# Second feed-forward product of an encoder layer: eight operand layouts and pass orders, chosen by K tile

## The chip, the core and the metric

The kernel runs on one core of a Trainium2 chip. The metric is the device time of one execution in microseconds (us). Before the change two runs gave 2583.47 and 2583.69 us, median 2583.58 us. One further execution was taken with the hardware profiler; its numbers are those of the profile below.

## The reference

One encoder layer on 2048 tokens of width 1024: an input projection, a bidirectional mLSTM group beside a latent attention group, an output projection, and a feed-forward block. Only the last line matters here:

```
h = rms_norm(x, g_ffn_norm[l])
x = x + jnp.square(jax.nn.relu(h @ w_ff1[l])) @ w_ff2[l]
```

`h` is 2048 x 1024, `w_ff1` 1024 x 4096, `w_ff2` 4096 x 1024. All is float32. The change touches the second product alone, the one with `w_ff2`.

## The kernel before, in words

**The program as a whole.** The phases follow one another: input projection, attention with the mLSTM scans woven in, output projection, first feed-forward product (`layer1`), second feed-forward product (`layer2`). Each float32 product is made from three matmuls of a rounded 32-bit type: every operand is split into a high part (a rounded copy, made by ACT, L53) and a low part (the difference, made by DVE, L54), and `mm3` (L68 to L71) issues high x high, high x low and low x high into the same PSUM bank. In the order of arguments of `nc.tensor.matmul(out, a, b)`, `a` is the stationary operand (128 columns, loaded by a LDWEIGHTS of its own) and `b` is the moving operand (up to 512 columns).

**The second product.** It is a seven-product scheme over 2 x 2 blocks of tokens and output columns (`PROD2`), so the main loop of `layer2` runs over `N = 7 * NU = 112` passes, with `NU = 16` K tiles to a product. Pass `n` has the product `i = n // 16` and the K tile `f = n % 16`. In one pass:

- the stationary operands are `uh` and `ul`, the two parts of a 128 x 2 x 512 tile of activations, cut into eight blocks of 128 tokens
- the moving operands are `wh` and `wl`, the two parts of a 128 x 512 tile of weights
- for each block `b` of 0 to 7 `mm3` adds three matmuls to the PSUM bank `pd[b]`; a bank is started in pass `f == 0` and stopped in `f == 15`, so a pass is 24 matmuls of 128 x 512 and a product 384.

**What runs beside it.** `load2(n + 3)` fetches the next raw tiles over SP's DMA queue, `combine2(n + 2)` lets POOL combine weight blocks in some products, and `split2(n + 2)` has ACT and DVE write the two parts of both operands, two passes ahead. The pools `g_u` and `g_w` hold three buffers, so the split for pass `n + 2` waits for the matmuls of pass `n - 1`. After the last pass of a product ACT and DVE copy the eight banks out (L1877, L1875) and DVE adds them to the accumulators (L1838) over the following passes. The order of issue is the order of the Python code here (a manual schedule): no planner moves anything.

**The places that the change touches.** `open2` (L1750) opens the pools and splits passes 0 and 1; `split2` (L1794) splits all later ones; the inner loop of `layer2` (around L1849) issues the matmuls. In all three `uh` and `ul` are tiles of `[P, 2, 512]` each, and `w2h` and `w2l` tiles of `[P, 512]`. Elements of all of them lie one after the other, and every matmul operand is a run of 128 or 512 neighbouring elements.

Of the kernel before, what the change touches and what calls it, by code (L numbers as in the profile page):

```python
# [9 lines left out]
F32R = mybir.dt.float32r  # L10
# [8 lines left out]
P = 128  # L19
# [30 lines left out]
def split(nc, hi, lo, src, g=None, eng=None):  # L50

    if g is None:
        r = nc.scalar.copy(hi, src)  # L53
        (eng or nc.vector).tensor_tensor(lo, src, hi.bitcast(F32), op=ALU.subtract)  # L54
    else:
        r = nc.scalar.activation(hi, src, AF.Copy, scale=g)
        nc.vector.scalar_tensor_tensor(lo, src, g, hi.bitcast(F32), op0=ALU.mult, op1=ALU.subtract)
    return r
# [9 lines left out]
def mm3(nc, out, ah, al, bh, bl, first, last):  # L68
    nc.tensor.matmul(out, ah, bh, start=first, stop=False)  # L69
    nc.tensor.matmul(out, ah, bl, start=False, stop=False)  # L70
    nc.tensor.matmul(out, al, bh, start=False, stop=last)  # L71
# [1378 lines left out]
class FeedForward:  # L1450
# [3 lines left out]
    NU = FF // 256  # L1454
# [295 lines left out]
    def open2(self, ent):  # L1750

        c, pool = self.c, self.c.tc.tile_pool
        self.urp = ent(pool(name="g_ur", bufs=4, reuse_waits="tile"))
        self.wrp = ent(pool(name="g_wr", bufs=4, reuse_waits="tile"))
        self.up = ent(pool(name="g_u", bufs=3, reuse_waits="tile"))
        self.wp = ent(pool(name="g_w", bufs=3, reuse_waits="tile"))
        self.R, self.acc, self.op2 = {}, {}, {}
        for n in range(2):
            r = self.raw2.pop(n)
            uh = self.up.tile([P, 2, 512], F32R, name="uh")  # L1760
            ul = self.up.tile([P, 2, 512], F32R, name="ul")
            wh = self.wp.tile([P, 512], F32R, name="w2h")
            wl = self.wp.tile([P, 512], F32R, name="w2l")
            for g in range(2):
                split(c.nc, uh[:, g, :], ul[:, g, :], r[g])
            split(c.nc, wh, wl, r[2])
            self.op2[n] = uh, ul, wh, wl
# [26 lines left out]
    def split2(self, n):  # L1794
        nc = self.c.nc
        ur, wr = self.raw2.pop(n)
        uh = self.up.tile([P, 2, 512], F32R, name="uh")
        ul = self.up.tile([P, 2, 512], F32R, name="ul")
        wh = self.wp.tile([P, 512], F32R, name="w2h")
        wl = self.wp.tile([P, 512], F32R, name="w2l")  # L1800
        split(nc, uh, ul, ur)
        split(nc, wh, wl, wr)
        self.op2[n] = uh, ul, wh, wl

    def load_acc(self, t):
        a = self.acc[t] = self.ap.tile([P, 2, 512], F32, name=f"acc{t}")
        self.c.nc.sync.dma_start(a.rearrange("p a n -> p (a n)"), self.c.d_x1[t * P:(t + 1) * P, :])
# [20 lines left out]
    def layer2(self, psD):  # L1828
        c, nc = self.c, self.c.nc
        NU = self.NU  # L1830
        N = 7 * NU
        todo = []

        def add(i, b, src, quad):
            a, j = quad
            t = 8 * (b // 4) + 4 * a + b % 4
            dst = self.acc[t]
            nc.vector.tensor_tensor(dst[:, j, :], src, dst[:, j, :], op=ALU.add)  # L1838
            tok = slice(t * P, (t + 1) * P)
            if i == 4:  # L1840
                self.later.append(lambda: nc.sync.dma_start(c.out[tok, :], dst.rearrange("p a n -> p (a n)")))
            elif i > 4:
                self.later.append(lambda: nc.sync.dma_start(c.out[tok, j * 512:(j + 1) * 512], dst[:, j, :]))

        for n in range(N):
            i, f = divmod(n, NU)
            if f == 0:
                pd = [psD.tile([P, 512], F32, name="pd") for _ in range(8)]
            uh, ul, wh, wl = self.op2.pop(n)  # L1849
            for b in range(8):  # L1850
                g, tt = divmod(b, 4)
                ts = slice(tt * P, (tt + 1) * P)
                mm3(nc, pd[b], uh[:, g, ts], ul[:, g, ts], wh, wl, f == 0, f == NU - 1)
            if n + 3 < N:
                self.load2(n + 3)
            if i == 0:
                self.load_acc(f)
            self.flush()
            if n + 2 < N:
                self.combine2(n + 2)  # L1860
                self.split2(n + 2)
            for _ in range(2):
                if todo:
                    todo.pop(0)()
            if f == NU - 1:
                while todo:
                    todo.pop(0)()
                quads = PROD2[i][2]
                for b in range(8):
                    if b % 2 and len(quads) == 1:  # L1870
                        add(i, b, pd[b], quads[0])
                    else:
                        t = c.e[:, b, :]
                        if b % 2:
                            nc.vector.tensor_copy(t, pd[b])  # L1875
                        else:
                            nc.scalar.copy(t, pd[b])  # L1877
                        for quad in quads:
                            todo.append(lambda i=i, b=b, t=t, quad=quad: add(i, b, t, quad))
                    if n == N - 1:  # L1880
                        while todo:
                            todo.pop(0)()
                        self.flush()
# [127 lines left out]
```

## Time and profile before

| what | value |
|---|---|
| median of two runs | 2583.58 us |
| span of the profiled execution, first to last instruction | 2586.2 us |
| PE busy with matmuls | 2567.1 us, 99% of the span |
| matmuls of the second product, out tile `pd` | 3 x 896 = 2688 |
| first of them, last of them starts | 1971.9 us, 2581.4 us |
| DVE, ACT, POOL busy | 1679.2, 1211.0, 402.9 us |

The profiled execution is 2.6 us longer than the median. In the profile PE stands for the matmuls, PEld for the loads of stationary operands, which overlap them. The duration given for one matmul holds its way through the array too, so that neighbouring matmuls overlap: what a matmul costs in a stream is the distance between two starts, its *pitch*. The profile names instructions by line; the matmuls of the second product stand at L69, L70 and L71 with the out tile `pd`.

### The profile page before, as it was taken

Reading aid. Unit: us, or ns where it says so; the run is one execution under the profiler, and the core shown is the slowest. Engines: PE = TensorE matmul, PEld = TensorE weight load, DVE = VectorE, ACT = ScalarE, POOL = GpSimd, SP = SyncE. Lnnn points to the kernel's source line nnn. Section 1 sums busy time; section 2 is a strip of 40 time slices with the busy share of each in tenths; the row PEclk is TensorE's granted clock in tenths of the full one; section 3 lists DMA queues with packets and bytes.
Section 4 is the critical chain, followed back from the end, with each engine's and each line's share of the span. In section 5 each row is a group of like instructions: output and inputs, shape, how many; then the busy total and the mean of one; then the engine's idle time right before and its main releaser. Section 6 shows DMA issues by size and latency. Waiting matters only on the chain. (4 is left out here: it accounts for less than half of the span.)

```text
span 2586.2 us, 37106 instructions
## 1 busy us (share of the span) xinstructions
PE 2567.1 (99%) x13232; PEld 2170.3 (84%) x13232; DVE 1679.2 (65%) x3206; ACT 1211.0 (47%) x2457; POOL 402.9 (16%) x438
## 2 busy tenths in 40 slices
PE   9999999999999999999999999999999999999999
PEld 7888888888888888898888888888888888888887
DVE  5585467666676667675448777877775577676443
ACT  5454444546656566561135554655554323332332
POOL 1211111023224224121000000000000233232000
PEclk9999999999999999999999999999999999999999
DMA  5434234356455555336675655744446644444652
GB/s 172 144 118 143 91 119 145 81 137 133 96 95 122 88 119 96 88 109 185 200 242 174 200 192 191 255 167 143 163 142 250 242 144 146 147 147 147 211 177 96
DMA packets 297757, 391.57 MB, mean 151 GB/s; under 512 B 32677, under 2 KB 186340, under 8 KB 297572
## 3 DMA queue, kind: packets, MB, share of 16 engines
q1 hardware_dynamic: 295108, 384.74, 49.7%
q10 hardware_dynamic: 2464, 4.46, 0.5%
q8 instruction: 104, 1.70, 0.3%
q14 instruction: 81, 0.66, 0.1%
HBM read 256.94 MB, written 132.17 MB: 150 GB/s over the span
## 5 line engine op out<-in xcount | busy, mean ns | idle before, releaser
L69 PE MATMUL pd<-w2h,uh 128*128 128x512 f32 x896 | 348.7, 389 | 0.1
L71 PE MATMUL pd<-w2h,ul 128*128 128x512 f32 x896 | 348.6, 389 | 0.0
L70 PE MATMUL pd<-w2l,uh 128*128 128x512 f32 x896 | 348.5, 389 | 0.0
L54 DVE TENSOR_TENSOR ul<-ur,uh 128x1024 fp32r<-128x1024 f32 x110 | 144.4, 1312 | 248.7 <-ACT uh L53 248.4
L53 ACT CAST uh<-ur 128x1024 fp32r<-128x1024 f32 x110 | 115.9, 1054 | 395.5 <-PE pd L70 381.0
L54 DVE TENSOR_TENSOR ptl<-ptp,pth 128x512 fp32r<-128x512 f32 x252 | 173.5, 689 | 171.5 <-ACT pth L53 166.5
L53 ACT CAST pth<-ptp 128x512 fp32r<-128x512 f32 x252 | 146.3, 582 | 244.9 <-PE ptp L1120 228.6
L1629 DVE TENSOR_TENSOR e<-pu,e 128x512 f32<-128x512 f32 x224 | 151.0, 687 | 96.0 <-PE pu L71 94.0
L1080 DVE TENSOR_SCALAR_CACHE_REDUCE p<-ps 128x512 f32<-128x512 f32 x256 | 174.6, 682 | 53.5 <-PE ps L1079 42.6
L69 PEld LDWEIGHTS pd<-w2h,uh 128*128 128x128 f32 x896 | 168.2, 188 | 35.4 <-DVE e L1629 0.5
L71 PEld LDWEIGHTS pd<-w2h,ul 128*128 128x128 f32 x896 | 168.2, 188 | 35.0
L70 PEld LDWEIGHTS pd<-w2l,uh 128*128 128x128 f32 x896 | 168.2, 188 | 34.9
L1789 POOL TENSOR_TENSOR r<-wr,r 128x512 f32<-128x512 f32 x48 | 92.2, 1920 | 614.5 <-DMA wr<-in_w 599.2
L1120 PE MATMUL ptp<-ident,p 128*128 128x128 f32 x1008 | 151.3, 273 | 0.7 <-ACT p L1091 0.7
L69 PE MATMUL pz<-wh,hh 128*128 128x512 f32 (+1 forms) x384 | 149.9, 392 | 2.1 <-ACT hh L53 1.1
L71 PE MATMUL pz<-wh,hl 128*128 128x512 f32 (+1 forms) x384 | 150.3, 391 | 0.0
L70 PE MATMUL pz<-wl,hh 128*128 128x512 f32 (+1 forms) x384 | 149.7, 391 | 0.1
L70 PE MATMUL pv<-ptl,vh 128*128 128x256 f32 x496 | 140.8, 284 | 2.3 <-DVE ptl L54 1.9
L69 PE MATMUL pv<-pth,vh 128*128 128x256 f32 x496 | 140.6, 284 | 0.4 <-ACT pth L53 0.4
L71 PE MATMUL pv<-pth,vl 128*128 128x256 f32 x496 | 140.3, 283 | 0.0
L1632 ACT ACTIVATE e<-e 128x512 f32<-128x512 f32 x128 | 81.0, 633 | 124.0 <-DVE e L1629 117.2
L1091 ACT ACTIVATE p<-p,nm 128x2048 f32<-128x2048 f32 x64 | 128.6, 2009 | 20.8 <-DVE nm L1084 20.2
(470 smaller groups left out, 6561.8 us busy)
## 6 DMA issues: line engine op xcount, KB each, us to landing
d_u<-e SPq DMA_DIRECT2D x224, 256.0 KB
ur<-d_u SPq DMA_DIRECT2D x110, 512.0 KB
wr<-in_w SPq DMA_DIRECT2D x96, 256.0 KB
w1raw<-in_w SPq DMA_DIRECT2D x42, 512.0 KB
raw<-in_w_in SPq DMA_DIRECT2D x48, 256.0 KB
r<-in_w SPq DMA_DIRECT2D x22, 512.0 KB
mb<-d_M SPq DMA_DIRECT2D x32, 256.0 KB
r<-in_x SPq DMA_DIRECT2D x16, 512.0 KB
```

What stands on the lines that cost most here:

```text
L53: r = nc.scalar.copy(hi, src)
L54: (eng or nc.vector).tensor_tensor(lo, src, hi.bitcast(F32), op=ALU.subtract)
L69: nc.tensor.matmul(out, ah, bh, start=first, stop=False)
L70: nc.tensor.matmul(out, ah, bl, start=False, stop=False)
L71: nc.tensor.matmul(out, al, bh, start=False, stop=last)
L1080: nc.vector.tensor_scalar(probs[b, a][:, j, :], o, SCALE, None, op0=ALU.mult, op1=ALU.max, accum_out=maxes[b, a][:, j:j + 1])
L1091: nc.scalar.activation(p, p, AF.Exp, bias=maxes.pop((b, a)), accum_out=dens[b][:, a:a + 1])
L1120: nc.tensor.transpose(pt[:, k, :], p[:, j, k * P:(k + 1) * P], c.ident)
L1629: nc.vector.tensor_tensor(out, o, t, op=ALU.add)
L1632: nc.scalar.activation(t, t, AF.Relu)
L1789: nc.gpsimd.tensor_tensor(R, wr, R, op=ALU.subtract)
```

## The change

The two parts of an activation tile now lie in one tile `u2` of 2064 elements to a partition (8256 bytes, where two tiles of 4096 bytes stood before), and each part of a weight tile in a tile of 528 elements (2112 bytes, before 2048). The K tile `f` picks a variant `v = f // 2`, 0 to 7, so each variant has 2 of the 16 passes of every product: 14 passes, 336 matmuls. The variants differ in one thing each:

| v | K tiles | what is different |
|---|---|---|
| 0 | 0, 1 | high part first, low part behind it, as runs of 1024 elements |
| 1 | 2, 3 | moving operand read from its last element to its first, and the PSUM output written in reverse too |
| 2 | 4, 5 | order within the pass: all eight blocks high x high, then all eight low x high, then all eight high x low |
| 3 | 6, 7 | high and low part interleaved element by element: both are written, and the stationary operand is read, with a step of 2 |
| 4 | 8, 9 | activation tile begins 8 elements (32 bytes) further on |
| 5 | 10, 11 | weight tiles begin 32 bytes further on |
| 6 | 12, 13 | weight tiles begin 4 elements (16 bytes) further on |
| 7 | 14, 15 | order within a block: high x low, high x high, low x high |

Its core:

```diff
     def split2(self, n):
         nc = self.c.nc
         ur, wr = self.raw2.pop(n)
-        uh = self.up.tile([P, 2, 512], F32R, name="uh")
-        ul = self.up.tile([P, 2, 512], F32R, name="ul")
-        wh = self.wp.tile([P, 512], F32R, name="w2h")
-        wl = self.wp.tile([P, 512], F32R, name="w2l")
+        v = n % self.NU // 2
+        uh, ul = self.place_u(v)
+        wh, wl = self.place_w(v)
         split(nc, uh, ul, ur)
         split(nc, wh, wl, wr)
         self.op2[n] = uh, ul, wh, wl
+
+    def place_u(self, v):
+
+        u = self.up.tile([P, 2064], F32R, name="u2")
+        if v == 3:
+            u = u[:, 0:2048].rearrange("p (g t a) -> p a g t", a=2, g=2)
+        else:
+            o = 8 if v == 4 else 0
+            u = u[:, o:o + 2048].rearrange("p (a g t) -> p a g t", a=2, g=2)
+        return u[:, 0], u[:, 1]
+
+    def place_w(self, v):
+
+        o = {5: 8, 6: 4}.get(v, 0)
+        return [self.wp.tile([P, 528], F32R, name=f"w2{part}")[:, o:o + 512] for part in "hl"]
+
+    def multiply2(self, n, pd):
+
+        nc, NU = self.c.nc, self.NU
+        f = n % NU
+        v = f // 2
+        uh, ul, wh, wl = self.op2.pop(n)
+        todo = []
+        for b in range(8):
+            g, tt = divmod(b, 4)
+            ts = slice(tt * P, (tt + 1) * P)
+            ah, al, o = uh[:, g, ts], ul[:, g, ts], pd[b]
+            bh, bl = wh, wl
+            if v == 1:
+                bh, bl, o = bh[:, ::-1], bl[:, ::-1], o[:, ::-1]
+            todo.append(((o, ah, bh), (o, ah, bl), (o, al, bh)))
+        order = [(b, i) for b in range(8) for i in range(3)]
+        if v == 2:
+            order = [(b, i) for i in (0, 2, 1) for b in range(8)]
+        elif v == 7:
+            order = [(b, i) for b in range(8) for i in (1, 0, 2)]
+        first, last = set(), {}
+        for b, i in order:
+            last[b] = i
+        for b, i in order:
+            nc.tensor.matmul(*todo[b][i], start=f == 0 and b not in first, stop=f == NU - 1 and last[b] == i)
+            first.add(b)
...
-            uh, ul, wh, wl = self.op2.pop(n)
-            for b in range(8):
-                g, tt = divmod(b, 4)
-                ts = slice(tt * P, (tt + 1) * P)
-                mm3(nc, pd[b], uh[:, g, ts], ul[:, g, ts], wh, wl, f == 0, f == NU - 1)
+            self.multiply2(n, pd)
```

`open2` gets the same two calls with `v = 0`. The number of instructions on every engine stays as it was; all matmuls of the second product now stand at one line, L1841, and those on the high and on the low part both read the tile `u2`.

On PE the first pass of variant 2 (K tile 4 of the first product) stands like this before. A row is line, operation, out tile, moving tile, stationary tile; `pd_20120` to `pd_20127` are the eight banks:

```order
L69 MATMUL pd_20120<-w2h_20236,uh_20234 128x512
L70 MATMUL pd_20120<-w2l_20237,uh_20234 128x512
L71 MATMUL pd_20120<-w2h_20236,ul_20235 128x512
L69 MATMUL pd_20121<-w2h_20236,uh_20234 128x512
L70 MATMUL pd_20121<-w2l_20237,uh_20234 128x512
L71 MATMUL pd_20121<-w2h_20236,ul_20235 128x512
```

And now, around the end of the second group of eight and the start of the third (the banks are `pd_20118` to `pd_20125`):

```order
L1841 MATMUL pd_20123<-w2h_20231,u2_20230 128x512
L1841 MATMUL pd_20124<-w2h_20231,u2_20230 128x512
L1841 MATMUL pd_20125<-w2h_20231,u2_20230 128x512
L1841 MATMUL pd_20118<-w2l_20232,u2_20230 128x512
L1841 MATMUL pd_20119<-w2l_20232,u2_20230 128x512
L1841 MATMUL pd_20120<-w2l_20232,u2_20230 128x512
```

Every matmul now goes to another bank than the one before it, and the moving tile changes once in the pass instead of sixteen times.

The first pass of variant 7 (K tile 14 of the first product) on PE, before:

```order
L69 MATMUL pd_20120<-w2h_20616,uh_20614 128x512
L70 MATMUL pd_20120<-w2l_20617,uh_20614 128x512
L71 MATMUL pd_20120<-w2h_20616,ul_20615 128x512
L69 MATMUL pd_20121<-w2h_20616,uh_20614 128x512
L70 MATMUL pd_20121<-w2l_20617,uh_20614 128x512
```

and now (`x2` are two such rows in a row):

```order
L1841 MATMUL pd_20118<-w2l_20602,u2_20600 128x512
L1841 MATMUL pd_20118<-w2h_20601,u2_20600 128x512 x2
L1841 MATMUL pd_20119<-w2l_20602,u2_20600 128x512
L1841 MATMUL pd_20119<-w2h_20601,u2_20600 128x512 x2
L1841 MATMUL pd_20120<-w2l_20602,u2_20600 128x512
```

The matmul with the low part of the weights comes first in each block; the banks are still finished one after the other.

More of the change, by code (lines that the diff above doesn't have):

```diff
@@ L1759, in open2 @@
             r = self.raw2.pop(n)
-            uh = self.up.tile([P, 2, 512], F32R, name="uh")
-            ul = self.up.tile([P, 2, 512], F32R, name="ul")
-            wh = self.wp.tile([P, 512], F32R, name="w2h")
-            wl = self.wp.tile([P, 512], F32R, name="w2l")
+            uh, ul = self.place_u(0)
+            wh, wl = self.place_w(0)
             for g in range(2):
@@ L1796, in split2 @@
         ur, wr = self.raw2.pop(n)
[L1797 to L1800, printed above, removed]
+        v = n % self.NU // 2
+        uh, ul = self.place_u(v)
+        wh, wl = self.place_w(v)
         split(nc, uh, ul, ur)
```

## The prediction

> **What bounds the kernel now.** I read the first page of the profile, then the view of the tile `pd`, then the timeline of one pass. The page comes first; its rows end with busy time, mean duration in ns, and the engine's idle time before such instructions:
>
> ```profile
> span 2586.2 us, 37106 instructions
> PE 2567.1 (99%) x13232; PEld 2170.3 (84%) x13232; DVE 1679.2 (65%) x3206; ACT 1211.0 (47%) x2457; POOL 402.9 (16%) x438
> L69 PE MATMUL pd<-w2h,uh 128*128 128x512 f32 x896 | 348.7, 389 | 0.1
> L71 PE MATMUL pd<-w2h,ul 128*128 128x512 f32 x896 | 348.6, 389 | 0.0
> L70 PE MATMUL pd<-w2l,uh 128*128 128x512 f32 x896 | 348.5, 389 | 0.0
> ```
>
> PE is busy for 99% of the span, and its 2688 matmuls of the second product were preceded by 0.1 us of idle time in all. Nothing that ACT, DVE, POOL or the DMAs do in this stage is late. How fast the matmuls stream is read from the view of `pd` (durations min/median/max in ns, then the first and last start):
>
> ```profile
> L69 PE MATMUL pd<-w2h,uh x896: 389/389/494, 1971.9 to 2580.9; 128*128 128x512 f32 x180
> L71 PEld LDWEIGHTS pd<-w2h,ul x896: 187/188/188, 1972.2 to 2581.2; 128*128 128x128 f32 x180
> L71 PE MATMUL pd<-w2h,ul x896: 388/389/397, 1972.4 to 2581.4; 128*128 128x512 f32 x180
> ```
>
> From the first start, 1971.9, to the last, 2581.4, are 2687 steps in 609.5 us: a pitch of 226.8 ns. A pass of 24 takes 5.44 us, and the 336 matmuls of one variant 76.2 us. The timeline inside one pass shows the same pitch without exception:
>
> ```profile
> 2100.18 0.39 PE L69 MATMUL pd<-w2h,uh 128*128 128x512 f32 x1
> 2100.19 0.19 PEld L70 LDWEIGHTS pd<-w2l,uh 128*128 128x128 f32 x1
> 2100.41 0.39 PE L70 MATMUL pd<-w2l,uh 128*128 128x512 f32 x1
> 2100.41 0.19 PEld L71 LDWEIGHTS pd<-w2h,ul 128*128 128x128 f32 x1
> 2100.64 0.39 PE L71 MATMUL pd<-w2h,ul 128*128 128x512 f32 x1
> 2100.64 0.19 PEld L69 LDWEIGHTS pd<-w2h,uh 128*128 128x128 f32 x1
> 2100.86 0.39 PE L69 MATMUL pd<-w2h,uh 128*128 128x512 f32 x1
> ```
>
> So the stage is a stream of matmuls with nothing between them. It changes its time only if the pitch of some matmuls changes, or if a split comes so late that PE waits. The granted clock gives no room; in this stretch PE, PEld, DVE and ACT (us, and counts), clock, DMA share and GB/s were:
>
> ```profile
> 2000.00:2100.00 100.00, 100.00 (x443) 82.81 (x442) 2.47 (x4) 2.35 (x4) 1.00 0.62 219
> ```
>
> **What a matmul's pitch is made of.** In the attention part matmuls of 256 columns stream, each with its own load of 128 columns:
>
> ```profile
> 1101.70 0.28 PE L69 MATMUL pv<-pth,vh 128*128 128x256 f32 x1
> ...
> 1102.89 0.28 PE L70 MATMUL pv<-ptl,vh 128*128 128x256 f32 x1
> ```
>
> Ten steps lie between these two, 1.19 us, a pitch of 119 ns. Another 256 columns cost 226.8 - 119 = 107.8 ns, so 0.421 ns a column: of the 226.8 ns, 215.6 ns are 512 columns and 11.2 ns are fixed. This gives a ceiling for any gain: if every matmul of the stage lost its whole fixed part, 2688 x 11.2 ns = 30.1 us, 1.2%. Faster by 2% (51.7 us) would need columns to go through faster, and every variant still moves 512 columns a matmul.
>
> **The change part by part**
>
> *Splits (all variants, and the step of 2 in variant 3).* One round of them, ACT and DVE (in brackets the idle time before and what ended it):
>
> ```profile
> 2102.88 1.05 ACT L53 CAST uh<-ur 128x1024 fp32r<-128x1024 f32 x1 [3.87 <-PE pd L70]
> 2103.96 1.23 DVE L54 TENSOR_TENSOR ul<-ur,uh 128x1024 fp32r<-128x1024 f32 x1 [1.32 <-ACT uh L53]
> 2105.11 1.78 DVE L54 TENSOR_TENSOR w2l<-r,w2h 128x512 fp32r<-128x512 f32 x1
> 2108.32 1.05 ACT L53 CAST uh<-ur 128x1024 fp32r<-128x1024 f32 x1 [3.87 <-PE pd L70]
> ```
>
> The round begins when the old pass has let go of its buffers, at 2102.88, and ends at 2106.89; it serves the pass two further on, which begins two passes, 10.88 us, after the start of the round: 6.9 us of slack. With `uh` and `ul` in one tile the release comes one matmul later (the last reader is then the low part), 0.23 us. If the step of 2 in variant 3 made the ACT copy and the DVE difference on 1024 elements four times as long, 3.15 and 3.69 us more, the round would still end inside its slack if nothing piled up, and only two passes in sixteen do it. Cost: 0, hidden behind 10.88 us of matmuls; without that cover it would be at most those 6.84 us in each of 14 passes, 96 us.
>
> *Orders (variants 2 and 7).* Each neighbourhood that they make has its kind in the timeline above: L69 to L70 keeps the stationary operand and changes the moving one, L70 to L71 changes both, L71 to L69 keeps the moving tile and changes bank and stationary operand. The starts lie 0.23, 0.23 and 0.22 us apart, rounded. So neither a change of bank nor one of the moving tile has a price here; 336 x 2 x 0 = 0. The read-out after K tile 15 meets the banks in the old sequence, since variant 7 still finishes block by block. The end of the kernel stays as it is, too: last matmul, read-out, last addition.
>
> *Start addresses and tile pitch (variants 4, 5, 6; and all variants, through the larger tiles).* No matmul operand of the trace is known by its row to begin 16 or 32 bytes off, but the rows do show pitches that differ with the place of the operands. In `layer1`, same shape:
>
> ```profile
> 1707.17 0.39 PE L69 MATMUL pu<-h0h,r 128*128 128x512 f32 x1
> ...
> 1709.74 0.39 PE L71 MATMUL pu<-h0h,r 128*128 128x512 f32 x1
> 1452.21 0.39 PE L71 MATMUL pu<-h2h,w1raw 128*128 128x512 f32 x1
> ...
> 1454.25 0.39 PE L71 MATMUL pu<-h2h,w1raw 128*128 128x512 f32 x1
> ```
>
> The first pair spans 11 steps, 233.6 ns each; the second 9 steps, 226.7 ns each. Moving tiles of the same pool, stationary tiles of another pool: 6.9 ns. That is the upper bound for a bad place: 336 x 6.9 ns = 2.3 us for each variant, 18.5 us if the larger tiles did it to all 2688. The lower bound is 0 for three of these, since 226.7 is the lower of the two pitches, or the fixed 11.2 ns at the very best, 3.8 us a variant. I take 0: the new tiles lie in the same pools in the same sequence, shifted by some hundred bytes, far nearer to the old ones than one pool is to another.
>
> *Stationary operand with a step of 2 (variant 3).* How long the load of an operand streams follows from two widths:
>
> ```profile
> L759 PEld LDWEIGHTS pm<-v,kw 128*64 128x64 f32 x240 | 12.5, 136 | 5.0 <-issue 5.0
> L71 PEld LDWEIGHTS pv<-pth,vl 128*128 128x128 f32 x496 | 94.7, 191 | 0.0
> ```
>
> With 188 ns for 128 columns (the row of `pd`) and 136 for 64, a column costs 0.81 ns, 128 columns 104 ns, and 84 are fixed. If a step of 2 halves the rate, a load takes 292 ns. Two ends follow. If the next matmul must wait for it as it seems to above (start of the load to start of its matmul 0.22 us, 0.03 us after its end), the pitch becomes 331 ns: 336 x 104 ns = 34.9 us. If loads overlap one another, only the 208 ns of streaming count, below 226.8: 0. The second row decides for me: there loads of 191 ns went by at a pitch of 119 ns, so a load may be longer than the pitch. I take 0 and keep 34.9 for the range. The Trainium skill, SBUF — State Buffer, in the box on cachelines under Door 1, says that full bandwidth needs two accesses to each 16-byte line; a step of 2 in 4-byte elements makes exactly two. By that rule variant 3 costs 0 as well; no run here shows it yet.
>
> *Reversed moving operand and output (variant 1).* The trace has no row of this kind. Below, the same 512 columns at 0.421 ns: 0. Above, the nearest I can price is half the column rate: 215.6 ns more for each of 336, 72.4 us. I take 0: the reversed stream touches the same words in the same neighbourhoods, only in the other direction. I hold this less firmly than the rest.
>
> The sum is 0 against the profiled span of 2586.2 us, so 0 against the median of the two runs, which is 2.6 us shorter: **2583.6 us**.
>
> **The rivals**
>
> 1. *Reversal halves the rate* (slower). Place: K tiles 2 and 3 of every product; mechanism: reading or writing downwards does not pair neighbouring elements, so a matmul takes 442 ns. It decides at once, since PE has no idle time to give: 2583.6 + 72.4 = 2656.0 us, 2.8% more. For it: no row has a downward step, and the stage has no cover. Against it: nothing in the rows ties the rate to a direction. The Trainium skill, PSUM — Partial Sum Buffer, Specifications, says that any access pattern to PSUM that is not contiguous slows matmuls significantly, with 8-byte lines; read literally this variant is such a pattern. No run here shows it so far.
> 2. *The stationary load with a step of 2 comes out from under the matmuls* (K tiles 6 and 7): 2583.6 + 34.9 = 2618.5 us. For it: in `pd` loads end only 0.03 us before their matmul. Against it: the loads of `pv`, longer than their pitch.
> 3. *The new places cost the 6.9 ns* seen between pools: from 2.3 us for one variant to 18.5 for all, 2585.9 to 2602.1 us.
> 4. *The change does less than it says*: PE runs every layout alike since an operand's pattern is resolved before it matters; the time is then the forecast's.
> 5. *Two or more of these prices, or a fourfold one, at once*: 2691 us and more (72.4 + 34.9 = 107.3).
>
> **How the numbers follow.** Within 2% is about what a measurement of this kernel can tell from no change, so the bounds are 2531.9 and 2635.3 us. Chances: forecast 0.59, rival 4 0.02, rival 3 0.12, rival 2 0.08, rival 1 0.15, rival 5 0.03, some unseen gain beyond 2% 0.01. Within 2% are the forecast and rivals 2 to 4: 0.81. Slower are rivals 1 and 5: 0.18. Faster 0.01, as the ceiling of 30.1 us forbids it. The likeliest case's own range is 2579.8 (one variant loses the fixed 11.2 ns) to 2590. The range to be held 8 times in 10 goes from 2579 to 2657: to leave out both rival 1 and rival 5 would be 0.18, but rival 2 and partial prices of the reversal lie in between, and 2656.0 is the bound of the one cost that no row covers.
>
> **What would show it.** All `pd` matmuls stand at one line then, so the steps are told apart by time: a product begins every 87.1 us, and each variant has 10.9 us of it. If I am right, the starts keep 226.8 ns in each of the eight stretches, PE's idle time before `pd` stays near 0, and the window rows count 443 matmuls in 100 us. A stretch of K tiles 2 and 3 with starts 0.44 us apart proves rival 1; loads much over 188 ns in K tiles 6 and 7 with starts over 0.23 us rival 2; 0.233 us in some stretches rival 3. Idle time on PE released by ACT or DVE would prove my slack wrong.

## The result, and the profile after

The changed kernel takes 2598.77 us (median of 2597.72 and 2599.82), against 2583.58 us: 15.2 us more, a ratio of 1.0058 with a 95% interval from 1.0042 to 1.0075. That is within 2%, and clear of noise. The page of the changed kernel, the rows that answer to those of before:

```profile
span 2595.9 us, 37103 instructions
PE 2578.3 (99%) x13232; PEld 2171.8 (84%) x13232; DVE 1678.5 (65%) x3206; ACT 1211.5 (47%) x2457; POOL 389.6 (15%) x438
L1841 PE MATMUL pd<-w2h,u 128*128 128x512 f32 x1792 | 545.3, 394 | 0.7 <-DVE e L1629 0.7
L1841 PE MATMUL pd<-w2l,u 128*128 128x512 f32 x896 | 337.6, 394 | 0.0
```

PE still waits for next to nothing (0.7 us before 2688 matmuls, at the start of the stage, for the phase before it). The view of `pd`, and one stretch of 100 us of those instructions alone (PE, PEld, DVE, ACT, then clock, DMA share, GB/s):

```profile
L1841 PE MATMUL pd<-w2h,u x1792: 388/394/499, 1967.0 to 2591.2; 128*128 128x512 f32 x200
```

```profile
2100.00:2200.00 100.00, 100.00 (x433) 81.32 (x432) 2.47 (x4) 2.34 (x4) 1.00 0.42 142
```

From the first start to the last are now 624.2 us where there were 609.5: the stage took 14.7 us more, at a mean pitch of 232.3 ns for 226.8, with 433 matmuls in 100 us instead of 443 and the same full clock. That is the whole difference. (The spans differ by only 9.7 us because the phases ahead of this stage took 4.9 us longer in the profiled execution of before: it reaches the stage at 1971.9 us, this one at 1967.0. So below the length of the stage is compared, or medians.)

Where the pitch grew is read from the starts of the 336 matmuls of each variant. Means in ns, worked out from the trace, first of the changed kernel, then of the two experiments that follow:

| variant | 0 straight | 1 reversed | 2 by groups | 3 step of 2 | 4 `u` +32 B | 5 `w` +32 B | 6 `w` +16 B | 7 order |
|---|---|---|---|---|---|---|---|---|
| the change | 230.1 | 233.4 | 233.1 | 230.4 | 233.1 | 231.8 | 233.5 | 230.2 |
| larger tiles alone, straight throughout | 230.2 | 230.0 | 230.1 | 230.2 | 230.0 | 230.1 | 230.2 | 230.0 |
| the change, tiles in steps of 512 B | 226.7 | 233.4 | 227.1 | 233.3 | 233.4 | 233.3 | 231.6 | 227.5 |

The first column leaves out the very first pass, which holds the one start-up wait of the stage. No variant of the change stands out: all eight cost 3 to 7 ns a matmul over the 226.7 of before, the straight one too.

### The profile page after: what moved, and what is told of

It is laid out like the page before. It is cut to its first block, busy times and chain, and to the rows that moved or that the text cites. A ratio compares the mean times of both kernels' runs of the same rounds, so it can differ in the third digit from the quotient of the medians.

```text
span 2595.9 us, 37103 instructions
## 1 busy us (share of the span) xinstructions
PE 2578.3 (99%) x13232; PEld 2171.8 (84%) x13232; DVE 1678.5 (65%) x3206; ACT 1211.5 (47%) x2457; POOL 389.6 (15%) x438
## 5 line engine op out<-in xcount | busy, mean ns | idle before, releaser
L1841 PE MATMUL pd<-w2h,u 128*128 128x512 f32 x1792 | 545.3, 394 | 0.7 <-DVE e L1629 0.7
L1841 PEld LDWEIGHTS pd<-w2h,u 128*128 128x128 f32 x1792 | 338.2, 189 | 78.7 <-DVE e L1629 1.1
L1841 PE MATMUL pd<-w2l,u 128*128 128x512 f32 x896 | 337.6, 394 | 0.0
L54 DVE TENSOR_TENSOR u<-ur,u 128x1024 fp32r<-128x1024 f32 x110 | 150.6, 1369 | 264.4 <-ACT u L53 264.4
L53 ACT CAST u<-ur 128x1024 fp32r<-128x1024 f32 x110 | 116.3, 1057 | 409.2 <-PE pd L1841 394.3
L1841 PEld LDWEIGHTS pd<-w2l,u 128*128 128x128 f32 x896 | 169.0, 189 | 38.6
L1787 POOL TENSOR_TENSOR r<-wr,r 128x512 f32<-128x512 f32 x48 | 78.6, 1638 | 635.6 <-DMA wr<-in_w 614.6
L1120 PEld LDWEIGHTS ptp<-ident,p 128*128 128x128 f32 x1008 | 120.7, 140 | 18.6 <-ACT p L1091 1.1
L1075 PE MATMUL ps<-kh,qh 128*128 128x512 f32 x256 | 123.7, 483 | 0.0
```

Of the source, the lines that this page charges most:

```text
L1075: nc.tensor.matmul(o, qh[:, qs], kh, start=True, stop=False)
L1120: nc.tensor.transpose(pt[:, k, :], p[:, j, k * P:(k + 1) * P], c.ident)
L1841: nc.tensor.matmul(*todo[b][i], start=f == 0 and b not in first, stop=f == NU - 1 and last[b] == i)
```

## The experiments

**The theory** that the table suggests: the pitch of a matmul depends on how its moving operand lies in the core's memory against the *stationary operand that is loaded meanwhile* (the next one). In the program before, both pools begin at the same remainder of 512 bytes (384) and all tiles are multiples of 2048 bytes long; tiles of 8256 and 2112 bytes move each buffer by another multiple of 64. Worked out from these sizes, the high weights of a pass then begin 192 bytes and the low weights 128 bytes after the activations, modulo 256, and this is so in all three buffers, since both pools advance by 64. **The rival**: each layout or order costs by itself, whatever lies beside it.

### The larger tiles alone

```diff
-        v = n % self.NU // 2
+        v = 0
...
-        v = f // 2
+        v = 0
```

> Only the larger tiles of the change (8256 and 2112 bytes to a partition), with the order and the straight layout of before in all 112 passes. Theory (place: a matmul's pitch depends on how its moving operand and the next stationary operand lie to each other, and the new tile sizes shift them by multiples of 64 bytes): every pass shows the 229 to 231 ns of variant 0 after the change, 3 to 4 ns over 226.8, so 2688 x 3.3 ns = 9 us more than before, about 2592.5 us. Rival (the variants: each reversal, step or offset costs on its own): all passes at 226.8 ns, 2583.6 us.

Measured: 2593.67 us beside 2584.44 for the kernel before, ratio 1.0035 (1.0020 to 1.0049). Every pass stands at 230 ns, and by the three buffers at 229.2, 229.8 or 231.3 in all sixteen K tiles. The row of 100 us, which had 443 matmuls before and 433 after the change:

```profile
2000.00:2100.00 100.00, 100.00 (x436) 81.67 (x435) 2.47 (x4) 2.34 (x4) 1.00 0.59 205
```

The same count of matmuls, order and layout as before, and the tile sizes alone cost 9.2 us. The rival's 2583.6 is excluded.

### The whole change, tiles in steps of 512 bytes

```diff
-        u = self.up.tile([P, 2064], F32R, name="u2")
+        u = self.up.tile([P, 2176], F32R, name="u2")
...
-        return [self.wp.tile([P, 528], F32R, name=f"w2{part}")[:, o:o + 512] for part in "hl"]
+        return [self.wp.tile([P, 640], F32R, name=f"w2{part}")[:, o:o + 512] for part in "hl"]
```

> The whole change, all eight variants, but with tiles of 8704 and 2560 bytes, multiples of 512 as before the change, so that only variants 4 to 6 shift the operands against each other. Theory (place): variants 0, 2 and 7 at 226.8 ns; 4, 5 and 6 at 230 to 235 ns, some 2 us each; 1 and 3 at 226.8 to 233 (a reversal and a step of 2 change which words meet, so they may cost up to 2.2 us each); in sum 4 to 10 us over before. Rival (the variants): the pitches of the change as it is, 230 to 233.5 ns, variant by variant, 14 us over before.

Measured: 2595.46 us, ratio 1.0044 (1.0029 to 1.0059), 11.0 us over before where at most 10 was expected. The third line of the table has what it was for. With the buffers back at one remainder, the straight variant has its 226.7 ns again, and the two orders cost next to nothing (227.1 and 227.5, and that only in their first steps, after a slow pass). Reversal, the step of 2 and the offsets still cost 5 to 7 ns a matmul each. So the orders are free, and the other five variants cost even in aligned buffers.

### Sweeps: one operand shifted, or both

The next two kernels use the straight order and those aligned tiles, and give each K tile an offset of its own (in elements of 4 bytes):

```diff
+    SHIFT = (0, 1, 2, 4, 8, 16, 24, 32, 48, 64, 80, 96, 112, 120, 124, 128)
...
-        o = {5: 8, 6: 4}.get(v, 0)
+        shift = {"h": self.SHIFT[v], "l": self.SHIFT[v]}
```

> Tiles of multiples of 512 bytes, straight order and layout; the weight tiles, high and low alike, begin 0, 4, 8, 16, 32, 64, 96, 128, 192, 256, 320, 384, 448, 480, 496 and 512 bytes on, one offset for each of the 16 K tiles. Theory (place): 226.8 ns at 0 and at 512, up to 235 ns in between, most within the first 64 bytes either way. Rival (the variants, an offset costs by its own alignment to 16, 32 or 64 bytes): 226.8 ns at all multiples of 64, more at 4, 8, 16, 32 and 496.

> As the sweep of the weight tiles, but the activation tile is shifted by the same offset, so that both operands keep their distance. Theory (place, relative): 226.8 ns at all 16 offsets, or a few ns at offsets that are no multiple of 16 bytes at most. Rival (alignment of each operand by itself): the same curve as in the sweep of the weight tiles.

Mean pitch in ns by offset in bytes, from the starts, again without the very first pass; one run each, 2599.52 and 2591.18 us:

| offset | 0 | 4 | 8 | 16 | 32 | 64 | 96 | 128 | 192 | 256 | 320 | 384 | 448 | 480 | 496 | 512 |
|---|---|---|---|---|---|---|---|---|---|---|---|---|---|---|---|---|
| `w` alone | 226.7 | 236.6 | 233.0 | 231.7 | 233.3 | 228.9 | 233.8 | 233.3 | 233.1 | 227.5 | 229.6 | 232.8 | 233.5 | 233.2 | 233.3 | 227.7 |
| `w` and `u` | 227.0 | 237.5 | 231.7 | 231.0 | 227.8 | 228.1 | 228.1 | 227.7 | 228.4 | 228.4 | 228.4 | 228.4 | 228.8 | 227.7 | 230.1 | 228.5 |

Shifted together by multiples of 32 bytes the two stay near 227 to 229 ns, and what is over 226.7 there stands at the borders of the passes, where the offset changes: from step 11 to 23 of a pass the mean is 226.7 at every one of these offsets. Shifted against each other they do not settle at 226.7, except by 256 or 512 bytes. The low weights of two neighbouring blocks are three steps apart; here are two such steps, twelve steps apart, in K tile 7 (128 bytes) of the third product, first with `w` alone shifted, 233 ns a step, then with both, 227 ns:

```profile
2189.57 0.40 PE L1843 MATMUL pd<-w2l,u 128*128 128x512 f32 x1
...
2192.37 0.40 PE L1843 MATMUL pd<-w2l,u 128*128 128x512 f32 x1
```

```profile
2185.67 0.39 PE L1843 MATMUL pd<-w2l,u 128*128 128x512 f32 x1
...
2188.39 0.39 PE L1843 MATMUL pd<-w2l,u 128*128 128x512 f32 x1
```

So at these offsets it is the distance that counts, and the means go in pairs 256 bytes apart: 64 and 320, 128 and 384, 192 and 448. The offsets of 4, 8, 16 and 496 bytes cost 3 to 11 ns even where both are shifted: there alignment matters as well, as the rival has it. Nor does the distance give the size of the cost: with the larger tiles alone the distances were 192 and 128 bytes, which cost 233 ns in this sweep, and the passes stood at 229.2 to 231.3 there, though in each pass the two distances came mixed. My expectation of a curve that is steep within 64 bytes and flatter beyond was wrong.

### Which two operands

```diff
+    SHIFT = tuple(range(0, 64, 4))
...
+        shift = {"h": 0, "l": self.SHIFT[v]}
```

> Tiles of multiples of 512 bytes, straight order and layout; only the low part of the weights is shifted, by 0, 16, 32 ... 240 bytes, one offset for each of the 16 K tiles. In a block the three steps are: high weights moving while the high activations are loaded again; low weights moving while the low activations are loaded; high weights moving while the next block's high activations are loaded. Theory (moving operand against the stationary operand that is loaded meanwhile): only the second step changes with the offset, 226.8 ns at 0 and up to 235 ns elsewhere; the first and the third stay at 226.8 ns in all 16 K tiles; in sum 2.5 to 5 us over before. Rival (one moving operand against the next one): the first two steps, at both borders between high and low weights, change alike.

2598.89 us in one run, 14 over the 2584.78 of before: neither theory as I had put it. All three steps of a block were slow at nearly all offsets, the third one too, in which no shifted operand is at work. Only at 240 bytes did the trace show what the theory says, 227.5, 233.1 and 226.7 ns. Two readings were left: the pair is another one, or a disturbed step unsettles the ones after it. The border between passes spoke for the second: in the sweep of `w`, at an offset of 256 bytes, the starts of a pass lie 237, 233, 230 and then 227 ns apart to its end. So the steps were grouped, by the order of variant 2, to give them time to settle; the second kernel shifts the low activations in place of the low weights:

```diff
-        if v == 2:
+        if v == 0:
             order = [(b, i) for i in (0, 2, 1) for b in range(8)]
...
+        o = self.SHIFT[v]
+        return [u[:, a:a + 1024].rearrange("p (g t) -> p g t", g=2) for a in (0, 1024 + o)]
```

> As the sweep of the low weights alone (0, 16 ... 240 bytes over the 16 K tiles), but every pass in the order of variant 2: steps 1 to 8 with high x high, 9 to 16 with low activations x high weights, 17 to 24 with high activations x low weights. Theory (a moving operand collides with the stationary operand loaded meanwhile, and a disturbed step unsettles the next few): steps 17 to 24 slow by an offset curve, 226.8 to 235 ns; steps 5 to 16 at 226.8 ns in all K tiles; about 4 to 5 us over before. Rival (one shifted operand spoils the whole pass, whatever reads beside it): steps 5 to 16 slow too, as in the sweep before, about 14 us over before.

> The same order by groups, weights not shifted, only the low part of the activations shifted by 0, 16 ... 240 bytes over the 16 K tiles: all moving operands begin at the same remainder, and the shifted operand is only ever loaded, while steps 8 to 15 run. Theory (moving operand against the operand loaded meanwhile): steps 8 to 15 slow by an offset curve, 226.8 to 235 ns; steps 1 to 7 and 20 to 24 at 226.8 ns, about 4 us over before. Rival (one moving operand against the next one): 226.8 ns in all steps of all K tiles, 0 over before.

One run each gave 2596.51 and 2595.47 us, beside 2584.65 for the kernel before. The timeline of a pass of the third product, first in the kernel that shifts the low weights (K tile 1, 16 bytes), then in the one that shifts the low activations (K tile 3, 48 bytes). Sixteen matmuls with the high weights, then eight with the low; a merged row gives its first start, its length and the count:

```profile
2152.06 3.79 PE L1843 MATMUL pd<-w2h,u 128*128 128x512 f32 x16
2155.69 2.01 PE L1843 MATMUL pd<-w2l,u 128*128 128x512 f32 x8
```

```profile
2163.06 3.84 PE L1839 MATMUL pd<-w2h,u 128*128 128x512 f32 x16
2166.74 1.98 PE L1839 MATMUL pd<-w2l,u 128*128 128x512 f32 x8
```

Less the last one's own 0.39 us, the first kernel has 227 ns in the sixteen and 231 in the eight, whose moving operand is shifted; the second has it the other way round, 230 in the sixteen, during which the shifted operand is loaded, and 227 in the eight. Step by step, means over products 2 to 7:

```
low weights shifted, 192 bytes:      230 235 229 232 231 227 226 227 | 227 226 227 227 226 227 227 226 | 234 233 233 234 233 233 234 233
low weights shifted, 16 bytes:       226 227 227 226 227 227 226 227 | 227 226 227 227 226 227 227 226 | 233 230 227 234 235 230 228 234
low activations shifted, 48 bytes:   227 226 227 227 226 227 227 232 | 234 233 234 233 234 232 234 227 | 227 226 227 227 226 227 227 226
low activations shifted, 128 bytes:  227 227 226 227 227 226 227 233 | 240 233 231 231 229 230 232 234 | 227 227 226 227 227 226 227 227
low activations shifted, 240 bytes:  227 226 227 227 226 227 227 226 | 227 226 227 227 226 227 227 226 | 227 226 227 227 226 227 227 226
```

This settles the pair, and the rows of 192 and 128 bytes weigh most, since shifting both operands by these amounts cost nothing once settled. With the low weights shifted, steps 17 to 24 are slow, in which they move; a few steps of the next pass are still unsettled, and from step 11 to 16 all K tiles are back at 226 to 228 ns. With the low activations shifted nothing that moves is shifted, so the border of two moving operands can't be the cause; yet at 48 and 128 bytes the starts stretch from step 8 on, the very step in which the first shifted block is loaded for step 9. The distance does not decide alone, though: low weights 240 bytes on and low activations 16 bytes on put the moving operand at the same distance from the loaded one, modulo 256, yet the first had steps 17 to 24 at 233 to 234 ns and the second was free.

Both stages grew more than I expected (618.6 and 617.1 us, 9.1 and 7.6 over 609.5, for 4 to 5 and 4): the unsettled steps cost more than I gave them, and some 1 us of it is an order that begins a product by groups. That is seen in K tile 0 of the third product in the second kernel, beside its K tile 9, which has the same 16 matmuls:

```profile
2145.78 4.70 PE L1839 MATMUL pd<-w2h,u 128*128 128x512 f32 x16
...
2196.15 3.79 PE L1839 MATMUL pd<-w2h,u 128*128 128x512 f32 x16
```

By groups, all eight banks are needed within eight steps, here before DVE has read them all out. Products 2 and 4 to 7 show no such wait. The change has this order at K tiles 4 and 5, where nothing is read out.

### Directions and steps, taken apart

```diff
+        w = self.wp.tile([P, 1280], F32R, name="w2")
+        if v in (3, 7):
+            return [w[:, 0:1024].rearrange("p (t a) -> p a t", a=2)[:, a] for a in range(2)]
+        o = 32 if v == 4 else 0
+        w = [w[:, o + k:o + k + 512] for k in (0, 640)]
+        return [x[:, ::-1] for x in w] if v in (1, 2, 4) else w
...
-            if v == 1:
+            if v in (2, 5):
                 bh, bl, o = bh[:, ::-1], bl[:, ::-1], o[:, ::-1]
```

> Tiles of multiples of 512 bytes and straight order; what the variants reverse or step is taken apart. K tiles 0, 1: straight. 2, 3: weights stored in reverse and read in reverse, output straight. 4, 5: stored in reverse, read straight, output in reverse. 6, 7: the two parts of the weights interleaved, read with a step of 2. 8, 9: as 2, 3, but 128 bytes on. 10, 11: moving operand and output reversed, as variant 1 of the change. 12, 13: activations interleaved, as variant 3. 14, 15: activations and weights interleaved. Theory (moving operand against the operand that is loaded meanwhile): the reversed read costs as much alone as in variant 1 (233.4 ns), the reversed output alone nothing (226.8 ns); steps of 2 cost 233 ns where only one operand has them. Rival (PSUM: a write downwards is what costs): 4, 5 at 233.4 ns and 2, 3 at 226.8.

One row of its timeline each for K tiles 1, 3, 5, 7, 9, 11, 13 and 15 of the third product, 24 matmuls in each. The pitch is the length less the last one's own duration (0.39 us, in the two long rows 0.63), over 23:

```profile
2195.74 5.60 PE L1840 MATMUL pd<-w,u 128*128 128x512 f32 x24
2206.79 5.76 PE L1840 MATMUL pd<-w,u 128*128 128x512 f32 x24
2217.84 5.60 PE L1840 MATMUL pd<-w,u 128*128 128x512 f32 x24
2234.14 11.06 PE L1840 MATMUL pd<-w,u 128*128 128x512 f32 x24
2250.72 5.84 PE L1840 MATMUL pd<-w,u 128*128 128x512 f32 x24
2261.99 5.76 PE L1840 MATMUL pd<-w,u 128*128 128x512 f32 x24
2273.19 5.76 PE L1840 MATMUL pd<-w,u 128*128 128x512 f32 x24
2289.66 11.06 PE L1840 MATMUL pd<-w,u 128*128 128x512 f32 x24
```

Reading the moving operand in reverse costs 233.4 ns alone (second row), what variant 1 costs as a whole (sixth); writing PSUM in reverse costs nothing (third, as the straight first). An offset of 128 bytes makes the reversed read worse, 237 (fifth). The step of 2 in the stationary operand costs 233.4 (seventh); its low part also begins 4 bytes on, and no run takes the two apart. And a step of 2 in the *moving* operand doubles the pitch, to 453 ns (fourth and eighth), which I had not expected: I had said 233. The kernel takes 2747.31 us in one run, 162.5 over before, nearly all of it in those four K tiles: 4 x 7 x 24 matmuls by 226.5 ns are 152 us.

### The same rule put to use in another phase

> The kernel before with one tile of another phase 64 bytes wider (280 instead of 264 elements), which moves all tiles of the right-hand stack of pools by 64 bytes, so that they begin at the same remainder of 512 (384) as those of the left-hand one, where they stood at 448. Nothing else is changed; the second product is untouched. Theory (place): in the first product the 768 matmuls with the moving tiles h0 to h2 and stationary tiles r, at 233 ns before, go to 226.8 ns: 768 x 6.5 ns = 5 us less, about 2578.6 us. Rival (only distance within the second product matters, or those 233 ns have another cause): no change, 2583.6 us.

```diff
-            y = op.tile([P, 264], F32, name="y")[:, 0:256]
+            y = op.tile([P, 280], F32, name="y")[:, 0:256]
```

The product that the prediction showed at 233.6 ns, same tiles, in this kernel:

```profile
1700.93 0.39 PE L69 MATMUL pu<-h0h,r 128*128 128x512 f32 x1
...
1703.42 0.39 PE L71 MATMUL pu<-h0h,r 128*128 128x512 f32 x1
```

Eleven steps in 2.49 us, 226.4 ns. The kernel takes 2577.28 us beside 2584.78, ratio 0.9970 (0.9959 to 0.9981): 64 bytes of padding make it 7.5 us faster than the kernel before, and so faster than both kernels. By groups of tiles the 768 matmuls give 5.0 us; another 1.8 us come from the score matmuls of the attention part, whose pitches fell by 2 ns, for which no run here isolates the cause.

## Why the prediction was right or wrong

The time lies in the stated range, but 15.2 us over the forecast and above the 2590 at which the forecast's own range ended. That the range held it says little for the forecast: it was drawn up to 2657 for the sake of rivals 1 and 2, which did not come, and covered rival 3 in passing. It is rival 3 that came, at 14.7 us of its 18.5.

- **The stream as the bound:** right. PE's idle time was 0.7 us, and the rest of the loss is pitch.
- **Splits at 0:** right. The DVE difference went from 1312 to 1369 ns on average, and nothing waits for it:

```profile
L54 DVE TENSOR_TENSOR u<-ur,u 128x1024 fp32r<-128x1024 f32 x110 | 150.6, 1369 | 264.4 <-ACT u L53 264.4
```

- **Orders at 0:** right in themselves (227.1 and 227.5 ns in aligned buffers). In the change they cost 233.1 and 230.2, in buffers in which the straight order costs 230.1 too. Why the order by groups costs 3 ns more there no run shows.
- **Start addresses and tile pitch at 0:** wrong, and this is the step that failed: "the new tiles lie in the same pools in the same sequence, shifted by some hundred bytes, far nearer to the old ones than one pool is to another". I took nearness for likeness, and the larger tiles alone cost 9.2 us. The 6.9 ns that I had quoted between two pools in `layer1` were themselves a shift of 64 bytes (448 against 384, modulo 512), as the last experiment shows by removing them. Read as "what differs between these pools", instead of as the bound for an unlikely case, that row gave 18.5 us beside the measured 14.7.
- **Step of 2 in the load at 0:** right on its own mechanism, wrong in the sum. The loads of variant 3 take a median of 194 ns in the trace for 188, far from 292, and stay hidden; the pitch nonetheless is 233.3 ns in aligned buffers, 2.2 us for the variant. That the stationary operand meets the moving one elsewhere is my reading of it, not shown by itself. Rival 2's 34.9 us did not come. The Trainium skill, SBUF — State Buffer, in the box on cachelines under Door 1, asks for two accesses to a 16-byte line for full bandwidth. The runs do not agree that this suffices: the step of 2 makes two such accesses, and cost 6.6 ns a matmul in the loaded operand and a factor of two in the moving one.
- **Reversal at 0:** the half rate of rival 1 did not come; the reversed read costs 6.6 ns a matmul, 2.2 us, and 10 ns when it lies 128 bytes further on. So its cost depends on its place too; whether a place exists where it is free no run shows. The reversed output is free at 226.7 ns. The Trainium skill, PSUM — Partial Sum Buffer, Specifications, lets any pattern that is not contiguous slow matmuls significantly. For an output written with a step of -1 the measured 226.7 ns differs, and decides.
- **Chances:** 0.59 went to the forecast and 0.12 to rival 3, which came. The bounds at 2% held, but they are no measure of what can be told from no change: the interval here, 1.0042 to 1.0075, excludes 1.

What stays open is the mechanism below the rule, and its sizes. That two reads of one memory collide, when one stream moves and one loads, would fit, but no run shows where they meet, why a step of 256 bytes is the period, why single offsets (16, 144 and 240 bytes for the loaded operand) are free, or why the same distances cost 3 ns in one kernel and 6 in another.

## What to carry to other kernels

Before changing a tile's size, look at where its buffers begin: here the remainder of the start modulo 256 bytes, moving operand against the stationary one that is loaded during it, was worth up to 7 ns of 227 in a matmul of 512 columns, with PE idle for no more than 0.7 us in the stage. Which remainders are bad has to be measured, since the distance alone did not give the cost. Where groups of matmuls of one shape differ by a few per cent in pitch and nothing waits, compare those remainders first; padding by 64 bytes on the other side of the memory was worth 7.5 us of this program. A step in the moving operand is no detail either: a step of 2 doubled the pitch here, while a reversed output cost nothing.

## What the runs showed of the hardware that was not expected

- A disturbed step is not paid for alone: in the sweeps the starts needed 3 to 10 further steps to come back to 226.7 ns (237, 233, 230, 227), and where one step in three was disturbed they did not come back at all at most offsets.
- A step of 2 elements in a moving operand of 32-bit elements takes the pitch from 226.7 to 453 ns for 512 columns; in a stationary operand to 233.4.
- An offset of 4 bytes gives 237.5 ns even where both operands have it, more than any other offset of that sweep.
